# A hybrid RWKV-7 / SGU / cross-attention block: regrouping the triangular solve, vector-engine precedence and a rebalanced final stretch

## The chip, the cores and the metric

One core of a Trainium2 chip runs the whole block. The metric is device time in microseconds (us). Its engines are TensorE (PE; the loading of its weights is listed apart as PEld), VectorE (DVE), ScalarE (ACT), GpSimd (POOL), and SyncE (SP), which here only issues DMAs. Each engine works through its own instruction stream in order. The kernel is written in a framework that orders the instructions of each engine at compile time: it picks among those that it thinks ready, by the order in which the program names them, unless a block is marked `high_priority`.

## The reference

One decoder layer over 1024 tokens of width 1024. Only the recurrent half matters here:

```
z  = rms_norm(x) @ w_in                    # one projection; SGU columns and RWKV columns
y1 = sgu_group(z_A)                        # gated unit, chunks of 128 tokens
y2 = rwkv7_group(z_B)                      # 8 heads of 64; per token:
     sa = state @ a                        #   a = -kk
     state = state*w + sa (x) (kk*icl) + v (x) k
     y = state @ r
     group norm, bonus, silu gate
h  = x + [y1, y2] @ w_out
h  = h + attention(rms_norm(h), rms_norm(mem))   # 4 heads, 256 memory tokens
out = rms_norm(h)
```

## The kernel before

Every large product is made of three matmuls (`mm3`, lines 177 to 179): operands are split into a rounded part and a remainder, written `_hi`/`_lo`. Three such matmuls with 512 moving columns are one "dense step". The input projection of the RWKV columns (`z_stream`) and the first part of the output projection (`out_proj`, tiles `wo`) are 321 dense steps, which serve as filler beneath the recurrence.

The recurrence works on eight half sequences `i` in turn (four pairs of heads, each in two halves of 512 tokens), each with eight chunks of 64 tokens. For one half:

- `elementwise` makes the decays, scaled keys `ra`, `bk` (DVE, ACT, a few matmuls).
- `grams` makes the 64x64 products of the chunks (line 655) in two groups of four chunks, masks them (DVE), writes them to DRAM (line 664), and reads back all 16x16 diagonal blocks (line 671). A chain of 28 small DVE operations (lines 676 and 678, tile `xtmp`) inverts these; the result goes through DRAM again and comes back as `t16` (lines 679 to 683).
- `turn` transposes `v` and `bk` per group of four chunks.
- `solve` joins the 16x16 inverses to 64x64 ones in five stages. Each is 16 matmuls of 64x64 by 64 (`pair_mm`, line 717) into a bank `cb`, with a DVE step between. The first stage also transposes the keys into `at` (line 728, copied by ACT at 729); the third also multiplies the values (`akv`). The last stage applies the inverse to `at` (bank `cb`) and to `akv` (bank `co`); ACT then copies the results to `ra` (line 747) and `avt` (750).
- `serial` is the recurrence over the chunks, two steps for each: state product `us` (line 773) and update of `avt` on DVE (774); then the state's update matmul (780) and two DVE operations for the new state `stdiag` (786). ACT copies `us` to `ytok` (789).
- `outputs` and `finish` make the output of a half; `finish` ends with the store of `y_scr` (line 829).

`drive` interleaves all that by hand. In phase `n` it runs the serial steps of half `n` at a planned pace, places the items of `grams(n+1)`, `turn`, `solve(n+1)`, `elementwise(n+2)` and `finish(n-1)` at fractions of the phase given by the windows `W_*` with planned costs `D_*`, and fills the rest with `n_dense` dense steps. Phases run from -2 to 7; a last `weave` puts 8 dense steps beside the last `finish`, and `drain(dense)` issues what is left, 11 steps. Then the tail begins: `k_fold` loads `w_qT` (line 959), which shares the SP queue and the pool's memory with what came before.

Of the kernel before, what the change touches and what calls it, by code (L numbers as in the profile page):

```python
# [10 lines left out]
F32 = mybir.dt.float32  # L11
F32R = mybir.dt.float32r
AF = mybir.ActivationFunctionType
ALU = mybir.AluOpType
# [4 lines left out]
P = 128  # L19
# [3 lines left out]
C = 64  # L23
NC = HT // C
# [7 lines left out]
W_G = (0.0, 0.13)  # L32
W_T0 = (0.28, 0.40)
W_Y0 = (0.56, 0.58)
W_T1 = (0.60, 0.70)
W_S = (0.66, 1.0)
W_E = (0.30, 0.98)
W_F = (0.08, 0.36)
D_BIG = 0.685
D_STEP = 0.235  # L40
D_HOP = (1.0, 1.35)
# [4 lines left out]
D_S = (2.2, 1.3, 2.2, 1.3, 2.2)  # L46
D_F = (0, 0, 0.46)
N_PROJ = (14, 28, 36)
# [34 lines left out]
def tile_hybrid_block(ctx: ExitStack, tc: tile.TileContext, x, xT, mem, memT, cst_d, vec_d, w_sv, w_blk, w2_d, a2_d,  # L83
# [14 lines left out]
    def co_ps():  # L98
        return psB.tile([P, 512], F32, name="co", bufs=2)

    def cb_ps():
        return psB.tile([P, 512], F32, name="cb")
# [353 lines left out]
    with tc.tile_pool(name="rw", bufs=1) as rw:  # L456
# [182 lines left out]
        def grams(i):  # L639
# [32 lines left out]
            nc.vector.tensor_tensor(out=X, in0=L.rearrange("p s t -> p t s"), in1=id16, op=ALU.add)  # L672
            for s in range(1, 15):
                m = 15 - s
                tmp = rw.tile([64, 56], F32, name="xtmp", bufs=2)[:, 0:m * s].rearrange("p (a b) -> p a b", a=m)
                nc.vector.tensor_tensor(out=tmp, in0=L[:, s, s + 1:16].unsqueeze(2).broadcast_to([64, m, s]),
                                        in1=X[:, s, 0:s].unsqueeze(1).broadcast_to([64, m, s]), op=ALU.mult)
                nc.vector.tensor_tensor(out=X[:, s + 1:16, 0:s], in0=X[:, s + 1:16, 0:s], in1=tmp, op=ALU.add)
# [26 lines left out]

        def solve(i):
# [3 lines left out]
            t16, ra = u["t16"], u["ra"]  # L710
# [13 lines left out]
            at = rw.tile([P, NC, C], F32, name="at")  # L724
# [3 lines left out]
            pa = pair_mm(co_ps(), lambda hh, c: ra[R[hh], c, 1, :], lambda hh, c: ident[R[hh], R[hh]])  # L728
            nc.scalar.copy(out=at, in_=pa)
# [15 lines left out]
            ps = pair_mm(cb_ps(), lambda hh, c: at[R[hh], c, :], lambda hh, c: tt[R[hh], c, :])  # L745
            pa = pair_mm(co_ps(), lambda hh, c: tt[R[hh], c, :], lambda hh, c: akv[R[hh], c, :])
            nc.scalar.copy(out=ra[:, :, 1, :], in_=ps)
            for j in range(2):
                for hh in range(2):
                    nc.scalar.copy(out=qs[j]["avt"][R[0], :, R[hh]], in_=pa[R[hh], QC * j:QC * j + QC, :])  # L750
            yield

        def serial(i):

            u = halves_u[i]
            ra, dc = u["ra"], u["dc"]
            u["y"] = ytok = rw.tile([P, 4, P], F32, name="ytok", bufs=2)
            for c in range(NC):
                q = quarters[2 * i + c // QC]
                avt, bkt, cq = q["avt"], q["bkt"], c % QC  # L760
                first = i % 2 == 0 and c == 0
                last = i % 2 == 1 and c == NC - 1
                n = state["i"]
                state["i"] += 1
                dcc = dc[:, c:c + 1]
                s_old, s_new = st_d[n % 2], st_d[(n + 1) % 2]
                us = psC.tile([P, 2, P], F32, name="us")
                yc = ytok[R[c % 2], c // 2, :]
                if first:
                    nc.gpsimd.memset(yc, 0.0)  # L770
                else:

                    nc.tensor.matmul(us[:, 0, :], ra[:, c, :, :], s_old, start=True, stop=True)  # L773
                    nc.vector.tensor_tensor(out=avt[R[0], cq, :], in0=us[R[1], 0, :], in1=avt[R[0], cq, :], op=ALU.add)
                    if not last:
                        sd = rw.tile([P, P], F32, name="sd")
                        nc.scalar.activation(out=sd, in_=s_old, func=AF.Copy, scale=dcc)
                yield
                if not last:
                    nc.tensor.matmul(us[:, 1, :], bkt[:, cq, :], avt[:, cq, :], start=True, stop=True)  # L780
                    for h2 in R:
                        if first:
                            nc.vector.tensor_scalar(out=s_new[h2, h2], in0=us[h2, 1, h2], scalar1=dcc[h2],
                                                    scalar2=None, op0=ALU.mult)
                        else:
                            nc.vector.scalar_tensor_tensor(out=s_new[h2, h2], in0=us[h2, 1, h2], scalar=dcc[h2],  # L786
                                                           in1=sd[h2, h2], op0=ALU.mult, op1=ALU.add)
                if not first:
                    nc.scalar.copy(out=yc, in_=us[R[0], 0, :])  # L789
                yield  # L790
# [104 lines left out]
        n_dense = {-2: 16, 5: 16 + N_PROJ[0], 6: N_PROJ[1], 7: N_PROJ[2]}  # L895

        def drive(steps, n_steps, others, n_big):
# [4 lines left out]
            pace = 0.97 * total / (max(n_steps, 1) / 2 * (sum(D_HOP) + 2 * D_STEP))  # L902
            t = ready = goal = 0.0
# [19 lines left out]
        with nullcontext():  # L923
            for n in range(-2, NH):
# [7 lines left out]
                    (ok(n + 2), lambda: elementwise(halves_u[n + 2]), D_E, W_E, 0),  # L932
                    (ok(n + 1), lambda: solve(n + 1), D_S, W_S, 0),
# [6 lines left out]
            weave([(outputs(2 * NH - 1), 1, 0.0, 0.0), (finish(halves_u[-1]), 3, 0.1, 0.5), (dense, 8, 0.0, 1.0)])  # L940
# [263 lines left out]
```

## Time and profile before

| | us |
|---|---|
| median of 3 runs | 960.01 (954.31 to 963.33) |
| profiled execution, its own time | 960.05 |
| its span, first to last instruction | 958.3 |
| PE busy | 926.8 (97%) |
| DVE busy | 582.0 (61%) |
| ACT busy | 396.3 (41%) |
| mean granted TensorE clock | 0.990 of full speed |

PE is busy nearly throughout; the recurrence lies between about 240 and 690 us. Matmuls overlap, so that the time from one start to the next says more than the duration of one. An `x32` behind a row counts instructions: each matmul on plain fp32 shows as two. A half's phase is named here by its place in the trace: phase 0 from 303 to 351 us, phase 1 from 351 to 400, phase 5 from 548 to 603, phase 6 to 650.5, phase 7 to 672, and behind it the stretch up to the tail's first matmul at 690.7.

### The profile page before, as it was taken

Reading aid. Unit: us, or ns where it says so; the run is one execution under the profiler, and the core shown is the slowest. Engines: PE = TensorE matmul, PEld = TensorE weight load, DVE = VectorE, ACT = ScalarE, POOL = GpSimd, SP = SyncE. Lnnn points to the kernel's source line nnn. Section 1 sums busy time; section 2 is a strip of 40 time slices with the busy share of each in tenths; the row PEclk is TensorE's granted clock in tenths of the full one; section 3 lists DMA queues with packets and bytes.
Section 4 is the critical chain, followed back from the end, with each engine's and each line's share of the span. In section 5 each row is a group of like instructions: output and inputs, shape, how many; then the busy total and the mean of one; then the engine's idle time right before and its main releaser. Section 6 shows DMA issues by size and latency. Waiting matters only on the chain.

```text
span 958.3 us, 17336 instructions
## 1 busy us (share of the span) xinstructions
PE 926.8 (97%) x6876; PEld 747.4 (78%) x6876; DVE 582.0 (61%) x1307; ACT 396.3 (41%) x802; POOL 49.6 (5%) x113
## 2 busy tenths in 40 slices
PE   6999999999999999999999999999899999999997
PEld 6978888888777777777777776777698778888885
DVE  5867233344674958586858698787677664433333
ACT  6753222225352526162526372435256653333222
POOL 0001000011000000000000000000000000000000
PEclk9999999999999999999999999899999999999999
DMA  9762011223121111111111174324462400000011
GB/s 318 256 213 80 31 66 66 68 72 109 36 58 36 40 23 50 35 51 30 52 32 43 27 211 148 101 60 141 150 211 70 123 22 1 23 23 23 28 39 44
DMA packets 86096, 76.93 MB, mean 80 GB/s; under 512 B 38272, under 2 KB 58752, under 8 KB 86016
## 3 DMA queue, kind: packets, MB, share of 16 engines
q1 hardware_dynamic: 84864, 73.73, 25.3%
q10 hardware_dynamic: 1152, 2.10, 0.6%
q8 instruction: 54, 0.88, 0.4%
q14 instruction: 26, 0.21, 0.1%
HBM read 62.17 MB, written 13.64 MB: 79 GB/s over the span
## 4 chain that ended last, share of the span: by engine, by line
PE 80%; DVE 8%; DMA 5%; ACT 3%; issue 3%; POOL 1%; POOLq 0%; SPq 0%; ACTq 0%; DVEq 0%
PE mm L177 21%; PE mm L179 20%; PE mm L178 20%; PE cb L717 4%; PE co L655 3%; PE co L717 2%; PE us L773 2%; PE us L780 1%; DMA w_raw<-y_scr 1%; PE yps L800 1%; POOL grs L153 1%; DMA w_raw<-in_w_sv 1%; DMA p_raw<-in_w_kv 1%; PE co L634 1%; PE co L432 1%
## 5 line engine op out<-in xcount | busy, mean ns | idle before, releaser
L177 PE MATMUL mm<-xh,w_hi 128*128 128x512 f32 x400 | 166.1, 415 | 0.0
L178 PE MATMUL mm<-xl,w_hi 128*128 128x512 f32 x400 | 160.0, 400 | 0.0
L179 PE MATMUL mm<-xh,w_lo 128*128 128x512 f32 x400 | 159.4, 398 | 0.0
L157 DVE TENSOR_TENSOR w_lo<-w_raw,w_hi 128x512 fp32r<-128x512 f32 x115 | 78.6, 686 | 62.0 <-ACT w_hi L156 61.3
L156 ACT CAST w_hi<-w_raw 128x512 fp32r<-128x512 f32 x115 | 70.9, 617 | 103.7 <-PE mm L178 90.6
L179 PEld LDWEIGHTS mm<-xh,w_lo 128*128 128x128 f32 x400 | 75.2, 188 | 15.6 <-issue 0.9
L177 PEld LDWEIGHTS mm<-xh,w_hi 128*128 128x128 f32 x400 | 75.3, 188 | 15.3 <-issue 2.1
L178 PEld LDWEIGHTS mm<-xl,w_hi 128*128 128x128 f32 x400 | 75.4, 188 | 14.2 <-issue 1.3
L177 PE MATMUL mm<-wo,w_hi 128*128 128x512 f32 x128 | 53.9, 421 | 0.0
L179 PE MATMUL mm<-wo,w_lo 128*128 128x512 f32 x128 | 53.0, 414 | 0.0
L178 PE MATMUL mm<-wo,w_hi 128*128 128x512 f32 x128 | 52.4, 409 | 0.0
L177 PE MATMUL mm<-vp_h,p_hi 128*128 128x512 f32 x128 | 51.3, 401 | 0.0
L498 ACT ACTIVATE t<-mm,vec 128x512 f32<-128x512 f32 x34 | 23.3, 687 | 65.0 <-PE mm L179 52.8
L179 PE MATMUL mm<-kp_h,w_lo 128*128 128x512 f32 x128 | 50.1, 391 | 0.0
L177 PE MATMUL mm<-kp_h,w_hi 128*128 128x512 f32 x128 | 50.0, 391 | 0.0
L179 PE MATMUL mm<-vp_h,p_lo 128*128 128x512 f32 x128 | 50.0, 390 | 0.0
L178 PE MATMUL mm<-vp_l,p_hi 128*128 128x512 f32 x128 | 49.9, 390 | 0.0
L178 PE MATMUL mm<-kp_l,w_hi 128*128 128x512 f32 x128 | 49.9, 389 | 0.0
L1041 DVE TENSOR_REDUCE mx<-mm 128x2 f32<-128x512 f32 x16 | 11.1, 691 | 41.8 <-PE mm L179 41.8
L655 PE MATMUL co<-ra,bk 64*64 64x128 f32 x512 | 35.5, 282 | 0.5 <-ACT avt L750 0.2
L786 DVE SCALAR_TENSOR_TENSOR stdiag<-us,dc,sd 64x64 f32<-64x64 f32 x112 | 31.7, 283 | 4.4 <-PE us L780 0.7
L789 ACT COPY ytok<-us 64x128 f32<-64x128 f32 x60 | 15.4, 256 | 43.6 <-DVE stdiag L786 34.1
(276 smaller groups left out, 2035.9 us busy)
## 6 DMA issues: line engine op xcount, KB each, us to landing
w_raw<-in_w_blk SPq DMA_DIRECT2D x50, 256.0 KB, 2.8
w_raw<-y_scr SPq DMA_DIRECT2D x32, 256.0 KB, 3.6
w_raw<-in_w_kv SPq DMA_DIRECT2D x17, 256.0 KB, 3.9
xr<-in_xT SPq DMA_DIRECT2D x8, 512.0 KB, 5.3
w_raw<-in_w_out SPq DMA_DIRECT2D x16, 256.0 KB, 2.8
h_all<-in_x SPq DMA_DIRECT2D x16, 256.0 KB, 5.0
pr<-in_w_qT SPq DMA_DIRECT2D x8, 512.0 KB, 4.5
w_raw<-in_w_o SPq DMA_DIRECT2D x16, 256.0 KB, 2.7
```

What stands on the lines that cost most here:

```text
L156: nc.scalar.copy(out=hi, in_=src)
L157: (eng or nc.vector).tensor_tensor(out=lo, in0=src, in1=hi.bitcast(F32), op=ALU.subtract)
L177: nc.tensor.matmul(ps, lh, rh, start=first, stop=False)
L178: nc.tensor.matmul(ps, lh, rl, start=False, stop=False)
L179: nc.tensor.matmul(ps, ll, rh, start=False, stop=last)
L498: nc.scalar.activation(out=t1[:, 1:HT + 1], in_=ps, func=AF.Copy, scale=vc("mu", b))
L655: nc.tensor.matmul(pss[hh][R[x], c, :, :], bk[R[hh], cc, x, :], ra[R[hh], cc, :, :], start=True, stop=True)
L717: nc.tensor.matmul(ps[R[hh], c, :], fl(hh, c), fr(hh, c), start=True, stop=True)
L773: nc.tensor.matmul(us[:, 0, :], ra[:, c, :, :], s_old, start=True, stop=True)
L786: nc.vector.scalar_tensor_tensor(out=s_new[h2, h2], in0=us[h2, 1, h2], scalar=dcc[h2], in1=sd[h2, h2], op0=ALU.mult, op1=ALU.add)
L789: nc.scalar.copy(out=yc, in_=us[R[0], 0, :])
L1041: nc.vector.tensor_reduce(out=m2, in_=ps.rearrange("p (h m) -> p h m", h=2), axis=AX.X, op=ALU.max)
```

## The change

- The solve's window begins earlier (`W_S` from 0.66 to 0.62), and the transposes of the keys become an item of their own, `keys`, due at 0.46 to 0.50 of the phase. `grams` is spread over 0.2 instead of 0.13 of the phase; `turn` and `finish` move a little.
- The 28 operations of the inverses' chain with the one ahead of them, the update of `avt` and the two of the state are marked `high_priority` on DVE.
- The last solve stage is written chunk by chunk with the two products interleaved; the second product's results go to the other half of the partitions, so that its four matmuls of a chunk lie in the four 64x64 quarters of the array.
- The planned serial steps begin 3.0 us into a phase (`D_START`).
- Dense steps: phases -2 and -1 get 20 and 28 (16 and 32 before), phase 7 gets 28 (36 before), the last weave 22 (8 before), `finish` there spans 0 to 0.65; 5 steps are left for the final drain.

```diff
-W_G = (0.0, 0.13)
-W_T0 = (0.28, 0.40)
+W_G = (0.0, 0.2)
+W_T0 = (0.20, 0.30)
-W_S = (0.66, 1.0)
+W_A = (0.46, 0.50)
+W_S = (0.62, 1.0)
-W_F = (0.08, 0.36)
+W_F = (0.10, 0.40)
+D_START = 3.0
-D_S = (2.2, 1.3, 2.2, 1.3, 2.2)
+D_A = (1.3,)
+D_S = (1.3, 1.3, 2.2, 1.3, 1.8)
-N_PROJ = (14, 28, 36)
+N_PROJ = (14, 28, 28)
...
+            with tc.high_priority():
+                nc.vector.tensor_tensor(out=X, in0=L.rearrange("p s t -> p t s"), in1=id16, op=ALU.add)
+                for s in range(1, 15):
...
+        def keys(i):
+            u = halves_u[i]
+            u["at"] = at = rw.tile([P, NC, C], F32, name="at")
+            ps = co_ps().rearrange("p (c t) -> p c t", c=NC)
+            for c in range(NC):
+                for r in R:
+                    nc.tensor.matmul(ps[r, c, :], u["ra"][r, c, 1, :], ident[r, r], start=True, stop=True)
+            nc.scalar.copy(out=at, in_=ps)
+            yield
...
-            pa = pair_mm(co_ps(), lambda hh, c: ra[R[hh], c, 1, :], lambda hh, c: ident[R[hh], R[hh]])
-            nc.scalar.copy(out=at, in_=pa)
...
-            ps = pair_mm(cb_ps(), lambda hh, c: at[R[hh], c, :], lambda hh, c: tt[R[hh], c, :])
-            pa = pair_mm(co_ps(), lambda hh, c: tt[R[hh], c, :], lambda hh, c: akv[R[hh], c, :])
+            ps, pa = [t.rearrange("p (c t) -> p c t", c=NC) for t in (cb_ps(), co_ps())]
+            for c in range(NC):
+                for r in R:
+                    nc.tensor.matmul(ps[r, c, :], at[r, c, :], tt[r, c, :], start=True, stop=True)
+                for hh in range(2):
+                    nc.tensor.matmul(pa[R[1 - hh], c, :], tt[R[hh], c, :], akv[R[hh], c, :], start=True, stop=True)
             nc.scalar.copy(out=ra[:, :, 1, :], in_=ps)
...
-                    nc.scalar.copy(out=qs[j]["avt"][R[0], :, R[hh]], in_=pa[R[hh], QC * j:QC * j + QC, :])
+                    nc.scalar.copy(out=qs[j]["avt"][R[0], :, R[hh]], in_=pa[R[1 - hh], QC * j:QC * j + QC, :])
...
+                    with tc.high_priority():
+                        nc.vector.tensor_tensor(out=avt[R[0], cq, :], in0=us[R[1], 0, :], in1=avt[R[0], cq, :],
+                                                op=ALU.add)
...
+                    with tc.high_priority():
+                        for h2 in R:
...
-        n_dense = {-2: 16, 5: 16 + N_PROJ[0], 6: N_PROJ[1], 7: N_PROJ[2]}
+        n_dense = {-2: 20, -1: 28, 5: 16 + N_PROJ[0], 6: N_PROJ[1], 7: N_PROJ[2]}
...
-            pace = 0.97 * total / (max(n_steps, 1) / 2 * (sum(D_HOP) + 2 * D_STEP))
-            t = ready = goal = 0.0
+            pace = (0.97 * total - D_START) / (max(n_steps, 1) / 2 * (sum(D_HOP) + 2 * D_STEP))
+            t, ready, goal = 0.0, D_START, D_START
...
+                    (ok(n + 1), lambda: keys(n + 1), D_A, W_A, 0),
...
-            weave([(outputs(2 * NH - 1), 1, 0.0, 0.0), (finish(halves_u[-1]), 3, 0.1, 0.5), (dense, 8, 0.0, 1.0)])
+            weave([(outputs(2 * NH - 1), 1, 0.0, 0.0), (finish(halves_u[-1]), 3, 0.0, 0.65), (dense, 22, 0.0, 1.0)])
```

## Rows read from the trace of the kernel before

**Rows 1.** The page's first part: busy time, share of span, instructions of each engine.

```profile
PE 926.8 (97%) x6876; PEld 747.4 (78%) x6876; DVE 582.0 (61%) x1307; ACT 396.3 (41%) x802; POOL 49.6 (5%) x113
```

**Rows 2.** Windows: stretch, length, busy us (instructions) by engine, PEclk, DMA share, GB/s.

```profile
303.00:351.00 48.00, 47.17 (x507) 35.31 (x504) 35.52 (x99) 19.75 (x46) 2.90 (x8) 1.00 0.15 37
...
548.00:603.00 55.00, 51.90 (x542) 38.96 (x541) 46.70 (x118) 27.88 (x60) 2.38 (x3) 1.00 0.58 171
...
650.50:672.00 21.50, 21.48 (x116) 16.15 (x116) 17.74 (x40) 11.67 (x28) 0.00 (x0) 1.00 0.52 150
```

**Rows 3.** Waits of PE: waiting line and releaser, us in total, times, longest.

```profile
PE mm L177 <- issue: 2.6, 1, 2.6
PE us L773 <- ACT ytok L789: 1.8, 4, 0.6
...
PE us L780 <- DVE avt L774: 1.2, 2, 0.7
PE co L717 <- ACT at L729: 1.0, 1, 1.0
```

**Rows 4.** Timeline of PE behind phase 7: start, duration; idle before in brackets.

```profile
679.80 0.63 PE L824 MATMUL yps<-cst,ytok 128*128 128x128 f32 x4 [0.97 <-DVE ytok L820]
...
690.72 0.55 PE L177 MATMUL mm<-ktt,p_hi 128*128 128x256 f32 x1 [2.59 <-issue]
```

**Rows 5.** Timelines of DVE, SP and ACT in the same stretch.

```profile
671.85 0.29 DVE L774 TENSOR_TENSOR avt<-us,avt 64x128 f32<-64x128 f32 x1
...
683.24 0.33 SPq L829 DMA_DIRECT2D y_scr<-ysq  x1
685.29 0.37 SPq L959 DMA_DIRECT2D pr<-in_w_qT  x1
...
690.00 1.14 ACT L156 CAST p_hi<-pr 128x512 fp32r<-128x512 f32 x2 [3.53 <-DMA pr<-in_w_qT]
```

**Rows 6.** Windows over the two stretches at the lower granted clock.

```profile
604.90:611.70 6.80, 6.80 (x40) 5.21 (x37) 4.72 (x12) 1.51 (x3) 0.00 (x0) 0.50 0.18 37
...
690.20:697.00 6.80, 6.29 (x22) 5.53 (x23) 3.85 (x7) 3.79 (x7) 0.00 (x0) 0.50 1.01 324
```

**Rows 7.** Timeline of DVE: the inverses' chain of phase 1, its start and end.

```profile
365.12 0.15 DVE L676 TENSOR_TENSOR xtmp<-ak,nt 64x14 f32<-64x14 f32 x1
365.31 0.29 DVE L786 SCALAR_TENSOR_TENSOR stdiag<-us,dc,sd 64x64 f32<-64x64 f32 x1
365.63 0.18 DVE L678 TENSOR_TENSOR nt<-nt,xtmp 64x14 f32<-64x14 f32 x1
...
380.19 0.16 DVE L678 TENSOR_TENSOR nt<-nt,xtmp 64x14 f32<-64x14 f32 x1
```

**Rows 8.** Timeline of PE: the solve's first piece in phase 1.

```profile
386.00 0.33 PE L717 MATMUL cb<-t,an 64*64 64x64 f32 x2
```

**Rows 9.** Timeline of PE: a last solve stage's first product, and what follows the second.

```profile
348.81 1.15 PE L717 MATMUL cb<-tt,at 64*64 64x64 f32 x32
...
350.82 0.49 PE L773 MATMUL us<-stdiag,ra 128*128 128x128 f32 x2
```

**Rows 10.** Timeline of PE: grams over four quarters, dense behind; grams of one bank.

```profile
263.16 1.33 PE L655 MATMUL co<-ra,bk 64*64 64x128 f32 x32
264.42 0.50 PE L177 MATMUL mm<-xh,w_hi 128*128 128x512 f32 x1
264.75 0.40 PE L178 MATMUL mm<-xl,w_hi 128*128 128x512 f32 x1
264.99 0.39 PE L179 MATMUL mm<-xh,w_lo 128*128 128x512 f32 x1
...
304.29 1.09 PE L655 MATMUL co<-ra,bk 64*64 64x128 f32 x16
```

**Rows 11.** The page's fifth part: all grams' matmuls; busy us, mean ns of one, idle before.

```profile
L655 PE MATMUL co<-ra,bk 64*64 64x128 f32 x512 | 35.5, 282 | 0.5 <-ACT avt L750 0.2
```

**Rows 12.** The chain that ended last: the keys' transposes of phase 0.

```profile
328.66 1.08 PE co L717 x32
```

More of the change, by code (lines that the diff above doesn't have):

```diff
@@ L671, in grams @@
             nc.sync.dma_start(out=L, in_=diag(ns))
[L672 to L678, printed above, removed]
+            with tc.high_priority():
+                nc.vector.tensor_tensor(out=X, in0=L.rearrange("p s t -> p t s"), in1=id16, op=ALU.add)
+                for s in range(1, 15):
+                    m = 15 - s
+                    tmp = rw.tile([64, 56], F32, name="xtmp", bufs=2)[:, 0:m * s].rearrange("p (a b) -> p a b", a=m)
+                    nc.vector.tensor_tensor(out=tmp, in0=L[:, s, s + 1:16].unsqueeze(2).broadcast_to([64, m, s]),
+                                            in1=X[:, s, 0:s].unsqueeze(1).broadcast_to([64, m, s]), op=ALU.mult)
+                    nc.vector.tensor_tensor(out=X[:, s + 1:16, 0:s], in0=X[:, s + 1:16, 0:s], in1=tmp, op=ALU.add)
             nc.sync.dma_start(out=diag(ti), in_=X)
@@ L704, in turn @@
             yield
+        def keys(i):
[7 more added lines that the diff above has]
+            yield
         def solve(i):
             u, qs = halves_u[i], quarters[2 * i:2 * i + 2]
-            t16, ra = u["t16"], u["ra"]
+            t16, ra, at = u["t16"], u["ra"], u["at"]
             of = lambda key, hh, c, rows: qs[c // QC][key][hh][rows, c % QC, :]
@@ L723, in solve @@
             akv = rw.tile([P, NC, C], F32, name="akv")
-            at = rw.tile([P, NC, C], F32, name="at")
             mk = lambda m, w: cs_(m)[:, 0:w].unsqueeze(1).broadcast_to([P, NC, w])
@@ L773, in serial @@
                     nc.tensor.matmul(us[:, 0, :], ra[:, c, :, :], s_old, start=True, stop=True)
-                    nc.vector.tensor_tensor(out=avt[R[0], cq, :], in0=us[R[1], 0, :], in1=avt[R[0], cq, :], op=ALU.add)
+                    with tc.high_priority():
+                        nc.vector.tensor_tensor(out=avt[R[0], cq, :], in0=us[R[1], 0, :], in1=avt[R[0], cq, :],
+                                                op=ALU.add)
                     if not last:
@@ L780, in serial @@
                     nc.tensor.matmul(us[:, 1, :], bkt[:, cq, :], avt[:, cq, :], start=True, stop=True)
[L781 to L787, printed above, removed]
+                    with tc.high_priority():
+                        for h2 in R:
+                            if first:
+                                nc.vector.tensor_scalar(out=s_new[h2, h2], in0=us[h2, 1, h2], scalar1=dcc[h2],
+                                                        scalar2=None, op0=ALU.mult)
+                            else:
+                                nc.vector.scalar_tensor_tensor(out=s_new[h2, h2], in0=us[h2, 1, h2], scalar=dcc[h2],
+                                                               in1=sd[h2, h2], op0=ALU.mult, op1=ALU.add)
                 if not first:
```

## The prediction

> **What bounds the kernel now.** I began with the page's busy shares: PE works 926.8 of 958.3 us [rows 1], so what isn't PE work is small. Next I read the windows, phase by phase [rows 2]. In phase 0 PE is busy 47.2 of 48 us, in phase 7 all 21.5; it loses 3.1 us in phase 5. The reader should see that neither DVE (35.5 of 48) nor ACT (19.8) is full, and that PE's idle time is under a microsecond except in phase 5 and, as the waits will show, behind phase 7. The list of PE's waits names the pieces [rows 3]: the largest in the recurrence is 2.6 us, once, put down to "issue", that is, to nothing the profile can name. The timeline places it ahead of the tail's first matmul at 690.72 [rows 4]. The other engines' timelines name its cause: `finish` stores `y_scr` at 683.24, only then is `w_qT` requested (685.29), and ACT begins to split it at 690.00, ended by that DMA [rows 5]. So the "issue" wait is a DMA wait that began with the last update of the recurrence at 671.85. The wait has a second price: from 690.2 the granted clock stands at 0.50 for 6.8 us, that is 1.2 instead of 2.4 GHz [rows 6]. At half speed that stretch does the work of 3.4 us, so 3.4 us are lost. The same happened once more, at 604.9 [rows 6], behind phase 5.
>
> In phases 0 to 4 two things last equally long, some 49 us. One is PE's work. The other is a loop: grams, DRAM, the chain of small DVE operations, DRAM, solve, then the next half's grams. In phase 1 the chain runs from 365.1 to 380.4 [rows 7] and the solve's first piece at 386.0 [rows 8]: 14, 29 and 35 us after the phase began. A gain on PE alone may therefore be taken back by the loop, and the other way round.
>
> **The change part by part.** *The final stretch.* From 671.85 to 690.72 are 18.9 us, the path from last update to `k_fold`; its links do not change. PE was idle for 0.97 + 2.59 = 3.6 us of it [rows 4] and worked 15.3. Behind the recurrence there were 8 + 11 = 19 dense steps and now there are 22 + 5 = 27. A dense matmul takes 0.24 us from start to start [rows 10], a step 0.7, so 8 steps are 5.6 us of cover where 3.6 were missing. But total work is unchanged; the gain comes only if phase 7, which gave up the 8 steps, gets shorter. It lasts 21.5 us for 8 chunks [rows 2], 2.7 each. One chunk needs matmul, DVE, matmul and two DVE operations after each other: 0.49 [rows 9] + 0.29 [rows 5] + 0.49 + 0.6 (two of 0.29 [rows 7]), in all 1.9 us without handoffs. Between 1.9 and 2.7 I take 2.3 (estimate): 18.4 us, 3.1 less. The path to `k_fold` then ends 3.1 earlier at 687.6, and PE has work to 671.85 + 15.3 = 687.2. Term: -3.1 (between 0 and -3.6). With 0.4 us of idle time instead of 2.6, PE no longer stops in front of the tail, and I expect the lower clock there to be gone: -3.4 (or 0).
>
> *The last solve stage in four quarters.* Before, its 64 instructions lie in two runs that take 350.82 - 348.81 = 2.01 us [rows 9], two quarters at work at any time. Whether four go together is shown by `grams`: 32 instructions over all four quarters took 1.33 us, 16 in one bank, over two quarters of one row half, took 1.09 [rows 10]. Without the last instruction's own 0.28 us [rows 11], that is 1.05 / 31 = 34 against 0.81 / 15 = 54 ns from start to start, a ratio of 0.63. Applied to the 1.73 us that 2.01 has beside such a run-out: 0.65 us less for each of 8 halves, -5.2 in all. At the other end, nothing: the runs of [rows 9] already start one instruction per 31 ns, about the 34 that four quarters reached. The nearest row by shape says -5.2, the nearest by rate says 0; I take the middle, -2.5. Against it stands that the copies to `ra` now begin only when both products are done. `D_START` puts dense work and grams there, so I cost that at nothing; without the cover it is one ACT copy, some 0.6 us per half.
>
> The Trainium skill's page "TensorE: Matmul & The Clock Gate", section "Wait — 56ns, not 53.3ns?", says that the time from start to start never falls below about 25 ns, however small the matmul. By it the stage could not take less than 64 x 25 ns = 1.6 us, so this term would end at -3.3. The rows do not show whether 34 ns is a floor of that sort; my -2.5 stays.
>
> *Keys on their own.* The transposes look new at their place, but the compiler had already moved them forward: in phase 0 they ran at 328.66 [rows 12], 0.53 of the phase, as a run by themselves. So `keys` adds no run of small matmuls to PE; each such run costs 0.1 us where dense work resumes (0.33 instead of 0.24 [rows 10]) and about as much where it stops, 1.6 us for eight if I am wrong. What it removes is the one wait on the copy to `at`, 1.0 us [rows 3]: -1.0.
>
> *Precedence for the chain.* The chain's 28 operations are short (0.15 to 0.18 us) yet it lasts from 365.1 to 380.4, 15 us [rows 7]. Between neighbours stands one operation of other work, not several: `xtmp`, `stdiag`, `nt`. What stands there is work that the program names later than the chain. So the chain already goes first; it alternates because its next operation is not yet ready when DVE comes free. Precedence cannot shorten that: 0. If it did, 28 x 0.18 = 5 us instead of 15 would bring `t16` 10 us earlier, of which only the idle time of a phase (0.8 in phase 0, 3.1 in phase 5) is time.
>
> *Precedence for the state's updates.* These lose to older work, and PE waits for them or for the copy behind them 1.8 + 1.2 = 3.0 us in six places [rows 3]. One operation in progress still has to end. I take a third: -1.0 (0 to -3.0; +1 if other DVE results come late instead).
>
> *The wider windows, `D_START`, the first phases' counts.* PE is full there, so moving filler changes nothing by itself: 0. What it costs if the loop decides is the last rival.
>
> Sum: -3.1 - 3.4 - 2.5 - 1.0 - 1.0 = -11.0. The profiled execution's own time is 960.05, equal to the median of 960.01 within 0.1, so 949.0 us.
>
> **The rivals.** *All quarters and the loop too:* four quarters reach their full ratio (-5.2 instead of -2.5), the clock also stays up behind phase 5 (-3.4 [rows 6]) because the solve's stages have more dense work between them, and the idle of phase 5 halves (-1.5): 960 - 11 - 7.6 = 941. For it: the mixed grams; against: the solve's first piece waits for `t16`, which nothing brings earlier. (If the skill's 25 ns hold, 943.)
>
> *Stalls only move:* the order of every engine is drawn anew from the compiler's times, which differ from the chip's; the six waits and the one on `at` reappear elsewhere, four quarters give nothing, and the tail's term alone stays, half of it lost: 960 - 3.2 = 957. For it: these waits are scattered and small, 0.3 to 1.0 us.
>
> *The loop becomes longer (slower):* the second group of grams is due at 0.10 of a phase instead of 0.065 (the third of five items in a window of 0.2 and 0.13). With some 45 us of planned work that is 1.6 us later, and DRAM, chain and solve follow it. Over the eight solves this is 13 us at the most. PE would use up dense steps ahead of time and lack them behind phase 7, where the path of 18.9 us would lie bare and the clock would fall as before. With 13 - 3.1 us the time is 970; with a delay of 1.3 per half, 967. It decides against the change from 0.4 us per half on, where 8 x 0.4 takes up the -3.1. For it: the solve's first piece is there only at 35 us of 49 [rows 8]. Against: the grams' masks, not the plan, seem to hold back the second group now.
>
> **How the numbers follow.** Forecast 949, with its own range 944 to 954: 0.50. Four quarters and loop, 941: 0.15. Stalls move, 957: 0.22. Longer loop, 967: 0.13. The range 939 to 963 leaves out about half of the last and the edges. A measurement of this kernel tells about 1% (9.6 us) from no change. Faster by over 1% means under 950.4: 0.6 of the forecast and all of the 941 case, 0.46; slower means above 969.6: 0.09 with room for mishaps; within 1%: 0.45.
>
> **What would show it.** In the profile after: no idle time above 1 us ahead of the first `ktt` matmul, and a granted clock of 1.0 there; phase 7 near 18 us; the last stage's 64 instructions in 1.4 to 2.0 us; the chain still 15 us long with one foreign operation between neighbours; no wait of PE on `at`. The forecast is wrong if the chain becomes short, if the solve's first piece comes later than 35 us into a phase, or if the dense steps run out before the store of `y_scr`.

## The result and the profile after

The change made the kernel slower: 990.94 us (986.23 to 995.59) against 958.41 (954.31 to 963.33), a ratio of 1.034 with the interval 1.026 to 1.041. The profiled execution took 992.92 us with a span of 991.1, so 32.8 us more than before's 958.3. The forecast was 949.0 and its range ended at 963.

The page's first part and the second part's rows of PE and of the granted clock (40 slices, in tenths), kernel after; they answer to [rows 1]:

```profile
PE 933.8 (94%) x6876; PEld 750.3 (76%) x6876; DVE 585.2 (59%) x1307; ACT 399.2 (40%) x802; POOL 51.7 (5%) x113
...
PE   6989999999999999999999898978879999999997
...
PEclk9999999999999999899999999998979999999999
```

PE is idle for 991.1 - 933.8 = 57.3 us, before for 31.5: 25.8 more. It is also busy 7.0 us longer, though the last solve stage now takes about 8.2 us less of it (below). Most of that difference is the clock, whose mean fell from 0.990 to 0.975. Windows of PE over all stretches at a granted clock of 0.50, their sum, kernel after (nine stretches) and before (four):

```profile
sum 49.50, PE 38.73; mean PE 4.30
sum 18.80, PE 16.48; mean PE 4.12
```

So 30.7 us more ran at half speed. Only busy time loses by that: (38.73 - 16.48) / 2 = 11.1 us. Then 25.8 idle + 11.1 clock - 8.2 stage = 28.7 of the 32.8 us; some 4 us of busy time stay without a cause.

The windows give the place. Columns as in [rows 2]; phases 0, 5, 6, 7 and the rest, kernel after:

```profile
305.80:355.60 49.80, 48.04 (x527) 37.01 (x527) 36.75 (x100) 20.88 (x46) 2.85 (x9) 1.00 0.15 40
...
569.50:635.30 65.80, 59.36 (x549) 44.95 (x547) 46.43 (x116) 24.59 (x54) 1.94 (x1) 0.95 0.35 99
635.30:681.90 46.60, 37.76 (x429) 30.17 (x430) 29.28 (x85) 14.67 (x35) 1.64 (x1) 0.85 0.19 48
681.90:705.90 24.00, 22.91 (x123) 17.59 (x122) 16.75 (x38) 9.92 (x25) 0.00 (x0) 1.00 0.38 113
705.90:984.10 278.20, 268.35 (x1313) 222.16 (x1312) 139.46 (x250) 110.85 (x232) 12.44 (x16) 0.98 0.18 60
```

Phases 0 to 7 run from 305.8 to 705.9 us, 400.1 us; before they took 303.5 to 671.3, 367.8. So 32.3 of the 32.8 us arise inside the recurrence. Phase 5 lasts 65.8 us, before 55 [rows 2]. Phase 6 is not longer (before 48.2, below), but PE works only 37.8 of its 46.6 us.

Phase 6 is empty because the filler was spent. Windows over line 181 (178 before), the second matmul of each dense step, so that its count is the number of steps; first phases 5 and 6 of the kernel after:

```profile
569.50:635.30 65.80, 16.92 (x40) 7.96 (x40) 0.95 0.35 99
635.30:681.90 46.60, 6.83 (x17) 3.20 (x17) 0.85 0.19 48
```

and the same phases of the kernel before:

```profile
547.60:602.20 54.60, 13.55 (x33) 6.23 (x33) 1.00 0.57 168
602.20:650.40 48.20, 12.60 (x30) 5.82 (x30) 0.93 0.28 76
```

The number of steps is fixed, and which of them stands in which phase is settled in the compiled order. There the longer phase takes more of them (40 for 33), and the last ones are missing where PE waits for the recurrence (17 for 30).

Which link of the loop became longer is read from DVE's timelines, from the first to the last of the chain's 28 rows [rows 7], in us:

| chain run in phase | before | after | no precedence | chain above the updates | eight products twice |
|---|---|---|---|---|---|
| 0 | 14.7 | 19.0 | 16.2 | 15.9 | 21.0 |
| 1 | 15.2 | 17.9 | 15.6 | 14.6 | 21.4 |
| 2 | 15.8 | 18.8 | 15.4 | 15.3 | 23.2 |
| 3 | 15.7 | 19.5 | 15.0 | 15.3 | 24.2 |
| 4 | 16.6 | 23.1 | 14.6 | 15.3 | 24.8 |
| 5 | 16.7 | 26.9 | 16.6 | 16.6 | 25.6 |
| sum with those in phases -1 and 6 | 119.6 | 150.2 | 118.6 | 116.9 | 173.1 |

(The last three columns are runs told below.) The chain is 30.6 us longer in sum, nearly the whole loss. The other links changed little: from the first gram to the chain's start 114.7 us in sum before and 116.9 after.

What makes it longer stands in DVE's timeline. Kernel after, the start of phase 5's chain (start, duration; idle before in brackets):

```profile
586.89 0.16 DVE L680 TENSOR_TENSOR xtmp<-ak,nt 64x14 f32<-64x14 f32 x1
586.98 0.68 DVE L618 TENSOR_TENSOR ra<-kk,E 128x512 f32<-128x512 f32 x1
587.78 0.58 DVE L806 SCALAR_TENSOR_TENSOR stdiag<-us,dc,sd 64x64 f32<-64x64 f32 x2
588.39 0.18 DVE L682 TENSOR_TENSOR nt<-nt,xtmp 64x14 f32<-64x14 f32 x1
588.48 0.68 DVE L625 SCALAR_TENSOR_TENSOR kk<-th,kk 128x512 f32<-128x512 f32 x1
589.08 0.17 DVE L680 TENSOR_TENSOR xtmp<-ak,nt 64x26 f32<-64x26 f32 x1
589.69 0.29 DVE L792 TENSOR_TENSOR avt<-us,avt 64x128 f32<-64x128 f32 x1 [0.43 <-PE us L790]
589.90 0.17 DVE L682 TENSOR_TENSOR nt<-nt,xtmp 64x26 f32<-64x26 f32 x1
590.11 0.42 DVE L822 TENSOR_TENSOR ytok<-ytok,yps 128x256 f32<-128x256 f32 x1
590.45 0.18 DVE L680 TENSOR_TENSOR xtmp<-ak,nt 64x36 f32<-64x36 f32 x1
590.63 0.58 DVE L806 SCALAR_TENSOR_TENSOR stdiag<-us,dc,sd 64x64 f32<-64x64 f32 x2
591.25 0.19 DVE L682 TENSOR_TENSOR nt<-nt,xtmp 64x36 f32<-64x36 f32 x1
```

Between the first two chain operations stand one operation of other work (`ra`) and, beside it, both updates of the state: 1.50 us for one step of the chain. Two operations on, the update of `avt` stands ahead of the chain although its product isn't there: DVE waits 0.43 us for PE and the chain waits with it. The Trainium skill, page "DVE: scalar operands, raw-bit mode, write accounting and state across instructions", section "5. Flops that outlive an instruction", calls DVE's queue one in-order queue; these rows agree, the chain's operation at 589.90 starts right behind the late `avt`. Such waits of DVE are, kernel after (us in total, times, longest):

```profile
DVE avt L792 <- PE us L790: 10.7, 17, 1.3
DVE stdiag L806 <- PE us L799: 8.6, 17, 1.1
```

and in the run without any precedence (told below):

```profile
DVE avt L790 <- PE us L789: 10.1, 14, 1.5
DVE stdiag L803 <- PE us L797: 8.1, 12, 1.2
```

Their total is nearly the same, so what counts is where they stand: inside the eight chains they make 4.2 us in the kernel after, 0.6 without precedence. And updates and waits are the smaller part. Between the first and the last operation of the chains DVE's rows are, after and without precedence: 87 and 71 updates (24.9 and 20.2 us), 142 and 111 operations of other work (86.9 and 68.0 us), and 15.3 and 8.0 us without a row. So of the chains' 31.6 us more some 19 are other, mostly long operations, which the new order puts between as well. Why the compiler puts them there no run shows.

### The profile page after: what moved, and what is told of

The parts are those of the page before. It is cut to its first block, busy times and chain, and to the rows that moved or that the text cites. A ratio compares the mean times of both kernels' runs of the same rounds, so it can differ in the third digit from the quotient of the medians.

```text
span 991.1 us, 17362 instructions
## 1 busy us (share of the span) xinstructions
PE 933.8 (94%) x6876; PEld 750.3 (76%) x6876; DVE 585.2 (59%) x1307; ACT 399.2 (40%) x802; POOL 51.7 (5%) x113
## 4 chain that ended last, share of the span: by engine, by line
PE 79%; DVE 6%; DMA 6%; ACT 4%; issue 3%; POOL 1%; SPq 0%; POOLq 0%; DVEq 0%; ACTq 0%
PE mm L180 21%; PE mm L181 20%; PE mm L182 20%; PE cb L732 4%; PE co L658 2%; PE us L790 2%; PE yps L820 1%; PE us L799 1%; DMA xr<-in_xT 1%; DMA t<-t_img 1%; DMA w_raw<-in_w_out 1%; DMA t_img<-nt 1%; DMA w_raw<-in_w_sv 1%; ACT avt L767 1%; PE co L717 1%
## 5 line engine op out<-in xcount | busy, mean ns | idle before, releaser
L180 PE MATMUL mm<-wo,w_hi 128*128 128x512 f32 x128 | 55.6, 434 | 2.8 <-ACT w_hi L159 1.7
L181 PE MATMUL mm<-wo,w_hi 128*128 128x512 f32 x128 | 53.9, 421 | 0.0
L806 DVE SCALAR_TENSOR_TENSOR stdiag<-us,dc,sd 64x64 f32<-64x64 f32 x112 | 31.7, 283 | 11.7 <-PE us L799 8.6
L1062 DVE TENSOR_REDUCE mx<-mm 128x2 f32<-128x512 f32 x16 | 11.1, 691 | 41.8 <-PE mm L182 41.8
L658 PE MATMUL co<-ra,bk 64*64 64x128 f32 x512 | 29.5, 274 | 5.7 <-DVE gr L668 4.0
L809 ACT COPY ytok<-us 64x128 f32<-64x128 f32 x60 | 15.4, 257 | 43.8 <-DVE stdiag L806 39.8
```

Source lines behind the costliest of these rows:

```text
L180: nc.tensor.matmul(ps, lh, rh, start=first, stop=False)
L181: nc.tensor.matmul(ps, lh, rl, start=False, stop=False)
L658: nc.tensor.matmul(pss[hh][R[x], c, :, :], bk[R[hh], cc, x, :], ra[R[hh], cc, :, :], start=True, stop=True)
L1062: nc.vector.tensor_reduce(out=m2, in_=ps.rearrange("p (h m) -> p h m", h=2), axis=AX.X, op=ALU.max)
```

## The experiments

Theory A: the precedence of the state's updates puts them, and DVE's waits for PE, between the chain's operations; the chain and with it each phase become longer, and the filler runs out. Rival B: the new windows, the start allowance or the counts do it. Rival C: the chain's own precedence does it. For C alone no run was needed: with precedence on the chain only, the compiled order of every engine is the same as with none. The other edits draw the order of all engines anew, so that none of them moves one thing alone. Each set of runs had its own runs of the kernel before, with medians from 956.2 to 957.3 us.

**Precedence taken away, halved, and put alone into the kernel before.**

The first run takes all three marks out of the changed kernel, the second only the chain's (the first mark below), the third puts all three into the kernel before and nothing else of the change. The first run's diff:

```diff
-            with tc.high_priority():
-                nc.vector.tensor_tensor(out=X, in0=L.rearrange("p s t -> p t s"), in1=id16, op=ALU.add)
+            nc.vector.tensor_tensor(out=X, in0=L.rearrange("p s t -> p t s"), in1=id16, op=ALU.add)
...
-                    with tc.high_priority():
-                        nc.vector.tensor_tensor(out=avt[R[0], cq, :], in0=us[R[1], 0, :], in1=avt[R[0], cq, :],
+                    nc.vector.tensor_tensor(out=avt[R[0], cq, :], in0=us[R[1], 0, :], in1=avt[R[0], cq, :],
...
-                    with tc.high_priority():
-                        for h2 in R:
+                    for h2 in R:
```

> The changed kernel without any precedence on the vector engine; windows, counts, keys and the last stage in four quarters stay. Theory A (precedence of the state's updates puts them, and the waits of the in-order vector engine for TensorE in front of them, between the operations of the inverses' chain): the chains of halves 1 to 6 go back from 17.9-26.9 us to 14.5-17 us each, the tail's first matmul comes near 680-692 instead of 723.5, and the time is 940-955 us. Theory B (the windows, the start allowance and the counts of projections did it): the chains stay at 18-25 us, and the time stays at 980-995. Theory C (the precedence of the chain itself did it): 940-955 as under A; the two runs with the updates' precedence alone tell A from C.

> The changed kernel with the precedence of the chain taken away and that of the state's updates kept. Theory A (the updates' precedence lengthens the chain): 985-996 us, like the changed kernel, chains of halves 1 to 6 at 18-27 us. Theory B (windows and counts): 980-995 too. Theory C (the chain's own precedence did it): 940-955 us.

> The kernel before with both precedences and nothing else of the change: its windows, counts, place of the keys and last stage. Theory A (the updates' precedence does it by itself): chains of halves 1 to 6 at 18-25 us instead of 14.7-16.7, 980-995 us. Theory B (the windows and counts did it): chains as before, 953-963 us. A value between, 965-978 us, would say that the precedence costs, and that the new windows or counts make it dearer.

Without precedence 956.97 us (ratio to before 1.000, 0.998 to 1.003), two above the range expected under A, chains at 118.6 us in sum. With the updates' precedence alone 988.70 (1.034, 1.030 to 1.038), chains 151.2. In the kernel before with precedence alone 985.75 (1.031, 1.028 to 1.035), chains 144.7. So the updates' precedence costs 988.7 - 957.0 = 31.7 us in the changed plan and about 29 in the old one (for 25.1 us of chain): the whole loss, and neither windows nor counts are needed for it. B and C fall. That 956.97 isn't under before shows too that the rest of the change gains nothing in sum, although the quarters do (next).

**The quarters alone.**

Into the kernel before goes the changed kernel's last stage and nothing else:

```diff
-            ps = pair_mm(cb_ps(), lambda hh, c: at[R[hh], c, :], lambda hh, c: tt[R[hh], c, :])
-            pa = pair_mm(co_ps(), lambda hh, c: tt[R[hh], c, :], lambda hh, c: akv[R[hh], c, :])
+            ps, pa = [t.rearrange("p (c t) -> p c t", c=NC) for t in (cb_ps(), co_ps())]
+            for c in range(NC):
+                for r in R:
+                    nc.tensor.matmul(ps[r, c, :], at[r, c, :], tt[r, c, :], start=True, stop=True)
+                for hh in range(2):
+                    nc.tensor.matmul(pa[R[1 - hh], c, :], tt[R[hh], c, :], akv[R[hh], c, :], start=True, stop=True)
```

> The kernel before with the last solve stage alone written over four quarters of TensorE's array; all else as before. The stage's 64 matmuls take 0.98 us in the changed kernel instead of 2.01, so 1.03 us for each of 8 halves. If that shortens TensorE's queue where it never waits, 950-953 us (8.2 us less); if the stage is only spread out, or the end of the recurrence is set elsewhere, 956-961 us (no difference).

951.02 us, ratio 0.9952 (0.9928 to 0.9976): 5.4 us less than before's 956.4 of the set. That is in the first of the two expected ranges, but not the full 8.2 us that it named. PE's time for the stage fell as in the changed kernel, whose timeline is (before: [rows 9]):

```profile
353.61 0.27 PE L761 MATMUL cb<-tt,at 64*64 64x64 f32 x2
353.62 0.27 PE L763 MATMUL co<-akv,tt 64*64 64x64 f32 x2
353.71 0.22 PE L761 MATMUL cb<-tt,at 64*64 64x64 f32 x2
...
354.54 0.22 PE L763 MATMUL co<-akv,tt 64*64 64x64 f32 x2
354.59 1.05 PE L658 MATMUL co<-ra,bk 64*64 64x128 f32 x16
```

64 records from 353.61 to 354.59 are 0.98 us in place of 2.01, 8 x 1.03 = 8.2 us for all halves; before, four of the eight stages took 1.92, so it is about 8.

**Which update.**

From the changed kernel one run takes the mark off the update of `avt` and keeps the state's; the other does the reverse:

```diff
-                    with tc.high_priority():
-                        nc.vector.tensor_tensor(out=avt[R[0], cq, :], in0=us[R[1], 0, :], in1=avt[R[0], cq, :],
+                    nc.vector.tensor_tensor(out=avt[R[0], cq, :], in0=us[R[1], 0, :], in1=avt[R[0], cq, :],
```

```diff
-                    with tc.high_priority():
-                        for h2 in R:
+                    for h2 in R:
```

> The changed kernel without the precedence of the update that makes avt; that of the two state updates (and of the chain) stays. Between the chain's operations the compiled order has 26 to 35 others in halves 1 to 6 (changed kernel 28 to 38, without precedence 23 to 27). Theory A goes by the chain's length: about half of the loss, 965-982 us. If the state's updates alone carry the loss, 983-993; if avt's does, 950-960.

> The changed kernel without the precedence of the two state updates; that of the update that makes avt (and of the chain) stays. The compiled order has 27 to 30 others between the chain's operations in halves 1 to 6. Theory A: a small loss, 956-966 us. If avt's precedence carries the loss, 975-992.

The state's: 974.67 us (1.017, 1.011 to 1.023), chains 136.8 in sum. The update of `avt`: 962.15 (1.005, 1.002 to 1.007), chains 126.2. Against the 956.97 and 118.6 without precedence that is +17.7 us for +18.2 us of chain, and +5.2 for +7.6; both together +31.7 for +32.6. The time follows the chain nearly one for one, and the two parts do not add up to the whole (22.9 of 31.7).

**The chain's precedence above the updates'.** One edit to the changed kernel:

```diff
-            with tc.high_priority():
+            with tc.high_priority(offset=1000000):
                 nc.vector.tensor_tensor(out=X, in0=L.rearrange("p s t -> p t s"), in1=id16, op=ALU.add)
```

> The changed kernel, with the one edit that the chain's precedence is given a far larger offset, so that it stands above the updates'; the updates keep theirs over all the rest. In the compiled order of the vector engine 25 to 27 other operations then stand between the chain's in halves 1 to 6, as in the kernel before (24 to 27), against 28 to 38 in the changed one. Theory A (the loss comes through the chain's length): chains of 14.5-17 us, and 945-958 us. Rival A2 (the updates' precedence costs through TensorE waits ahead of the vector engine's other work, evictions and outputs, whatever the chain does): 975-992 us.

953.13 us, ratio 0.9961 (0.9936 to 0.9985): the loss is gone though the updates keep their precedence over all else. DVE's timeline at the start of this run's chain of phase 5, the same six operations of the chain:

```profile
559.37 0.16 DVE L680 TENSOR_TENSOR xtmp<-ak,nt 64x14 f32<-64x14 f32 x1
559.46 0.68 DVE L160 TENSOR_TENSOR w_lo<-w_raw,w_hi 128x512 fp32r<-128x512 f32 x1
560.06 0.17 DVE L682 TENSOR_TENSOR nt<-nt,xtmp 64x14 f32<-64x14 f32 x1
560.26 0.28 DVE L806 SCALAR_TENSOR_TENSOR stdiag<-us,dc,sd 64x64 f32<-64x64 f32 x1
560.46 0.17 DVE L680 TENSOR_TENSOR xtmp<-ak,nt 64x26 f32<-64x26 f32 x1
560.66 0.29 DVE L806 SCALAR_TENSOR_TENSOR stdiag<-us,dc,sd 64x64 f32<-64x64 f32 x1
560.98 0.18 DVE L682 TENSOR_TENSOR nt<-nt,xtmp 64x26 f32<-64x26 f32 x1
...
562.57 0.18 DVE L682 TENSOR_TENSOR nt<-nt,xtmp 64x36 f32<-64x36 f32 x1
```

Again one operation between neighbours, the two updates split over two gaps: 562.57 - 559.37 = 3.20 us where the kernel after took 591.25 - 586.89 = 4.36. Rival A2, that the updates' waits cost by themselves, falls with it for this plan.

**The chain's length by itself, both ways.**

Both start from the run with the quarters alone; one makes eight products twice, the other does seven of fourteen steps and leaves the inverses unfinished:

```diff
-                nc.vector.tensor_tensor(out=tmp, in0=L[:, s, s + 1:16].unsqueeze(2).broadcast_to([64, m, s]),
+                for _ in range(2 if 4 <= s < 12 else 1):
+                    nc.vector.tensor_tensor(out=tmp, in0=L[:, s, s + 1:16].unsqueeze(2).broadcast_to([64, m, s]),
```

```diff
-            for s in range(1, 15):
+            for s in range(1, 8):
```

> The kernel before with the last stage in four quarters and no precedence, where eight of the chain's products are made twice (the same value twice into the same tile), so that each chain has 36 operations in place of 28, with 35 to 36 others between them in the compiled order. Theory A (what costs is a longer chain, whatever makes it long): chains of halves 1 to 6 at 20-24 us, 30-40 us more in sum, and 978-992 us in place of 951.0. Rival A2 (what costs is the updates' waits for TensorE, and a chain that is longer by work alone is covered by TensorE's other work): 950-962.

> The kernel before with the last stage in four quarters, where the chain does only its first seven of fourteen steps (the other products and sums are left out, so the inverses are unfinished): chains of about 6-8 us in place of 15.5, some 55-60 us less in sum. If the recurrence follows the chain's length in both directions: 890-905 us. If TensorE's own work bounds it as soon as the chain is as short as in the kernel before (its idle time in the recurrence is about 11 us in all): 940-951.

The longer chain, with no precedence anywhere: 1008.0 us (1.055, 1.050 to 1.059), slower than expected; its chains are 173.1 us in sum, 54.0 more than the 119.1 of the run with the quarters alone, and the time 57.0 more. Its windows show the same picture as the kernel after, phases 3 and 6:

```profile
474.70:532.80 58.10, 57.03 (x555) 43.70 (x555) 40.21 (x114) 24.60 (x53) 4.19 (x11) 1.00 0.17 41
...
652.70:703.60 50.90, 37.91 (x393) 29.28 (x394) 28.64 (x90) 15.03 (x35) 1.64 (x1) 0.63 0.21 55
```

PE is full in phase 3 (with filler) and starved in phase 6, at a clock of 0.63. The short chain: 938.4 us (0.981, 0.977 to 0.985), 12.6 less than 951.0 for chains of 5 to 9 us instead of 15 to 17 (61.9 less in sum); under the expected 940, but far from 890. Windows over phases 0 to 7, first of the short chain:

```profile
299.50:645.50 346.00, 330.93 (x3701) 261.01 (x3702) 262.85 (x645) 160.04 (x352) 17.92 (x47) 1.00 0.26 71
```

then of the run with the quarters alone:

```profile
302.40:666.70 364.30, 350.38 (x3696) 266.93 (x3697) 275.65 (x748) 160.62 (x354) 17.86 (x45) 0.99 0.26 70
```

PE is busy 96% of both. So before the change the kernel stood near the bend: above a chain of some 15 us each further us is about a us of time, below it a fifth of one. What bounds it below is not shown: the same work of PE (3701 and 3696 rows) is busy for 331 us in one and 350 in the other, so a busy PE is not PE at its limit, and with the short chain the serial steps end only 2 to 5 us ahead of the solve, with the quarters alone 15 to 18.

**Counts and windows.**

From the changed kernel without precedence one run puts back the counts of before:

```diff
-N_PROJ = (14, 28, 28)
+N_PROJ = (14, 28, 36)
...
-        n_dense = {-2: 20, -1: 28, 5: 16 + N_PROJ[0], 6: N_PROJ[1], 7: N_PROJ[2]}
+        n_dense = {-2: 16, 5: 16 + N_PROJ[0], 6: N_PROJ[1], 7: N_PROJ[2]}
...
-            weave([(outputs(2 * NH - 1), 1, 0.0, 0.0), (finish(halves_u[-1]), 3, 0.0, 0.65), (dense, 22, 0.0, 1.0)])
+            weave([(outputs(2 * NH - 1), 1, 0.0, 0.0), (finish(halves_u[-1]), 3, 0.1, 0.5), (dense, 8, 0.0, 1.0)])
```

The next puts back the windows too:

```diff
-W_G = (0.0, 0.2)
-W_T0 = (0.20, 0.30)
+W_G = (0.0, 0.13)
+W_T0 = (0.28, 0.40)
...
-W_S = (0.62, 1.0)
+W_S = (0.66, 1.0)
...
-W_F = (0.10, 0.40)
+W_F = (0.08, 0.36)
...
-D_START = 3.0
+D_START = 0.0
```

From this last one three runs undo one part each: `W_G` and `W_T0`; `D_START`; `W_S` and `W_F`.

> The changed kernel without precedence, and with the counts of the kernel before (16 and 32 projections in the first two stretches, 36 in the last phase, 8 in the final stretch, finish at its old place); windows, keys and last stage stay changed. The kernel before with the quarters alone took 951.0 us and the changed kernel without precedence 957.0. If the counts of the final stretch cost these 6 us, 950-953; if the windows or the keys do, 955-959.

> The changed kernel without precedence, with the counts and also the windows of the kernel before for the grams, the first turn, the solve stages and finish, and without the start allowance; only the keys' own step and the last stage in quarters stay. Before with the quarters alone took 951.0 us; with the new windows and keys 957.8. If the windows cost the 6 us, 949-953; if the keys' own step does, 955-959.

> The run with the old windows (keys' own step and quarters, no precedence, 950.4 us) with one edit: the changed kernel's windows for the grams (0 to 0.2) and the first turn (0.20 to 0.30). The prediction's rival of a delayed second group of grams says that the chain starts later in each half: 954-958 us if these windows carry the 7 us by which all new windows together are slower (957.8), 949-952 if they carry nothing.

> The run with the old windows (950.4 us) with one edit: the start allowance of 3.0 for the serial steps. They begin later and end nearer to the end of each phase; if that carries the 7 us of the new windows, 954-958, with the last serial run of phase 7 ending later against its start (20.6 us with the old windows, 23.3 with all the new ones); if not, 949-952.

> The run with the old windows (950.4 us) with one edit: the changed kernel's windows for the solve stages (0.62 to 1.0) and finish (0.10 to 0.40). 954-958 us if these carry the 7 us of the new windows, 949-952 if not.

With the counts of before 957.83 us against 956.97 with the new ones: no difference that can be told. With the old windows too 950.44 (0.993, 0.991 to 0.995): the windows cost about 7 us, and the keys' own step, which stays in this run, nothing (951.02 without it). The grams' window alone gives 957.28 (1.001, 0.998 to 1.005), the solve's 955.75 (1.000, 0.998 to 1.002), the start allowance 947.45 (0.991, 0.987 to 0.994): two cost, one is 3 us lower, under both of its expected ranges, and they don't add up. That gain is not clear of noise, its interval overlaps with that of 950.44. If it is real, the compiled order has a reason that fits theory A: with serial steps begun later 8 or 9 of the updates stand between a chain's operations in phases 0 to 5, without 9 to 11, and the chains are 115.6 us in sum for 118.8. For the two losses no cause is shown. The chain doesn't begin 1.6 us later in each half with the grams' window: from the first gram to the chain 116.9 us in sum against 114.8. In the profiled execution with the solve's window, 951.52 us, nothing is lost at all.

**The updates' precedence below the chain's, in the old plan.**

The three marks, the chain's with the large offset, go into the run with the quarters alone and into the one with the old windows:

```diff
+            with tc.high_priority(offset=1000000):
+                nc.vector.tensor_tensor(out=X, in0=L.rearrange("p s t -> p t s"), in1=id16, op=ALU.add)
...
+                    with tc.high_priority():
+                        nc.vector.tensor_tensor(out=avt[R[0], cq, :], in0=us[R[1], 0, :], in1=avt[R[0], cq, :], op=ALU.add)
...
+                    with tc.high_priority():
+                        for h2 in R:
```

> The kernel before with the last stage in four quarters, the updates' precedence, and the chain's above theirs by a far larger offset; windows, counts and keys as before. Theory A: the chains stay at 14.5-17 us (25 to 27 others between in the compiled order), and the updates' precedence by itself is worth what it was worth in the changed plan, 3-4 us (957.0 to 953.1): 945-951 us. If the updates' precedence is worth nothing in this plan: 949-954. If it costs by anything but the chain: over 960.

> The run with the old windows (keys' own step, last stage in quarters, counts of before; 950.4 us) with the updates' precedence, and the chain's above it by the large offset. In the new plan this precedence was worth 4 us (957.0 to 953.1), in the plan of before with quarters under 1 us (951.0 to 950.4): 946-951 us.

950.45 us (0.993, 0.990 to 0.995) where 951.02 stood without, and 955.89 (0.999, 0.996 to 1.001) where 950.44 stood, against the expectation. With the gain of 3.8 in the new plan the updates' precedence below the chain's is worth -3.8, -0.6 and +5.5 us: it has no value of its own. The loss of 5.5 does not come through the chains, which are 120.3 us in sum for 118.8; its cause is open, and so theory A holds for the loss of some 30 us and not for every difference of 5. Among the runs with the whole chain the one with the start allowance, old windows and no precedence is the lowest, 947.45 us; several others at 950 to 951 beat both kernels too.

## Why the prediction was wrong, point by point

**The step that failed: precedence of the state's updates, -1.0 (0 to -3.0; +1).** Measured: +31.7. The updates did what was meant: from the second product's end to the state's first update the 80th percentile of DVE's delay fell from 0.86 to 0.28 us in the timelines. But nothing waited for that: in phase 1 before, the serial steps ran from 350.8 to 382.5 while the solve ended only at 399, 16 us of slack (the time by which the serial steps end ahead of the solve); in phases 0 to 6 it is 15.5 to 18.8 us. With the precedence the serial steps of phase 1 took 27.4 us for 31.7, and the slack grew to 25.7. The term's upper bound was priced by PE's listed waits [rows 3]; the price was on DVE, and the "other DVE result" that came late was the chain, 30.6 us in sum. I had named loop and chain as the second bound and then didn't ask who stands behind the updates on DVE.

**Precedence for the chain, 0.** Right for this edit (no engine's order changes). The sentence behind it, that the chain already goes first and alternates with one operation, was a state that the next edit destroyed: in the compiled order 28 to 38 operations stand between the 28 of a chain in phases 0 to 5, before 24 to 27. The priced aside, that a shorter chain is worth only the idle time of a phase, holds roughly: 12.6 us for half a chain.

**The final stretch, -3.1, and its clock, -3.4.** Neither came. Kernel after, last update (DVE), store and requests (SPq), ACT's split, and PE, answering to [rows 4, 5], from four timelines in this order; DVE:

```profile
705.91 0.29 DVE L792 TENSOR_TENSOR avt<-us,avt 64x128 f32<-64x128 f32 x1 [1.08 <-PE us L790]
```

SP's queue:

```profile
716.61 0.33 SPq L849 DMA_DIRECT2D y_scr<-ysq  x1
718.67 0.37 SPq L980 DMA_DIRECT2D pr<-in_w_qT  x1
```

ACT:

```profile
722.79 1.14 ACT L159 CAST p_hi<-pr 128x512 fp32r<-128x512 f32 x2 [2.96 <-DMA pr<-in_w_qT]
```

PE:

```profile
713.62 0.63 PE L844 MATMUL yps<-cst,ytok 128*128 128x128 f32 x4 [1.69 <-DVE ytok L840]
...
723.50 0.55 PE L180 MATMUL mm<-ktt,p_hi 128*128 128x256 f32 x1 [7.71 <-DMA w_raw<-y_scr]
```

The path from the last update is 17.6 us, before 18.9, but PE lacks work for 1.69 + 7.71 = 9.4 of it. Phase 7 took 24.0 us, not 18.4. Windows over the two longest stretches at half clock, late in the starved phase 6 and here, answering to [rows 6]:

```profile
665.00:678.70 13.70, 8.88 (x133) 7.90 (x133) 5.16 (x9) 2.63 (x4) 1.55 (x1) 0.50 0.35 100
719.60:729.90 10.30, 6.39 (x23) 5.64 (x24) 4.30 (x8) 3.86 (x8) 0.00 (x0) 0.50 0.95 303
```

That the dense steps run out before the store of `y_scr` was a sign named for a wrong forecast, and it came. So did the late solve: its first piece stands 36.4 to 51.1 us into phases 0 to 5, before 33.5 to 40.1. Freed of the updates' precedence the term fails as well: in that run the path is 18.8 us, PE's timeline shows

```profile
687.95 0.36 PE L180 MATMUL mm<-ktt,p_hi 128*128 128x256 f32 x1 [2.07 <-issue]
```

2.07 us idle for 2.59, now at full clock, and the counts of before change the time by 0.9 us only; 6.5 us were expected. The clock is not shown to be the cover's doing: the run with the quarters alone has the old counts, and its clock there is 1.00 too. What failed is the count of 27 steps of cover. Windows over the second matmul of a dense step, from the last update to the first `ktt` matmul, before, without precedence, and after:

```profile
671.85:690.70 18.85, 7.02 (x18) 3.38 (x18) 0.99 0.37 110
669.10:687.90 18.80, 7.52 (x19) 3.56 (x19) 1.00 0.35 98
705.91:723.45 17.54, 3.13 (x8) 1.50 (x8) 0.89 0.22 73
```

There are 18 steps before, 19 without precedence and 8 after: the plan's count is not the compiled order's, and the cover never came. Nor did phase 7 become shorter: without precedence it lasts 22.3 us, with 21 of these matmuls for 23.

**Last stage in four quarters, -2.5 (0 to -5.2).** The direction held, the size was too small. PE needs 8.2 us less for it, and the run alone shows 5.4. The rate of 34 ns from the grams was no floor: the stage reaches 15 ns a record. The rule of the Trainium skill weighed there (page "TensorE: Matmul & The Clock Gate", section "Wait — 56ns, not 53.3ns?"), applied to the 64 records, gave at least 1.6 us; the trace has 0.98, so applied that way it does not hold here. By written matmuls, two records each, the rate is 31 ns, and no run here shows which of the two the rule counts. Another section of that page, "Measured speedup vs the span model", counts some 4 ns of issue time for each further tile. In the trace of the kernel after the records of the four quarters start 7 ns after each other, and the next four 58 ns later.

**Keys, -1.0.** PE's wait on `at` is gone from the list; in time 950.44 against 951.02, not to be told from nothing.

**Windows, start allowance, first counts: 0.** Wrong by +7 us for the windows together, with +7, +5 and -3 (not clear of noise) for their parts by themselves. "PE is full there" was no reason: what they move is the order on every engine.

**The rival of the longer loop (0.13, 967)** had the right course: the loop grows, dense steps are spent early and missing behind phase 7, the clock falls. Its cause, later grams, was not it (116.9 against 114.7 us from grams to chain in sum). Its price was bounded by a delay in the plan, 1.6 us a half; the chain gave 3 to 10.

## What to carry over

Before giving an instruction precedence on an in-order engine, ask what slack its result has and which dependent chain on that engine will stand behind it; price each slot, each wait in front of it and the other work that the new order lets in, by the loop that the chain belongs to. Precedence on work with slack costs whoever has none; if it is given at all, the chain without slack must stand above it. A loop that just fits under its filler looks harmless in the waits of the busy engine: test it by making it longer.

## What the runs showed that was not expected

The time follows the chain's sum nearly one for one upwards (+57.0 us for +54.0, +31.7 for +32.6) and hardly downwards (-12.6 for -61.9); the plans' differences of 5 to 7 us at an equal sum it does not explain. And a spent stock of filler has a second price: in the two emptiest stretches PE ran 24.0 us at half clock, where the kernel before had 6.8 us ahead of its tail [rows 6]. In all the lower clock cost about 11 us of PE's work, beside 25.8 us more of idle time.
